# Eight more U blocks held in idle places, the residual and the group sum moved towards the end, and row shares 45, 26, 35, 30

## The chip, the cores and the metric

The kernel runs on one core of a Trainium2 chip. Its time is device microseconds of one execution, taken as the median of several runs. A profile of one further execution shows what each engine did: PE is the matrix engine (PEld its weight loads), DVE the vector engine, ACT the scalar engine, POOL the GpSimd engine, and SP the sync engine, which here only issues transfers. SPq and ACTq are the two queues from which SP and ACT issue plain transfers; gathers are issued by POOL on a third queue. A transfer stands in its engine's program like any other instruction: if the instruction ahead of it waits, it waits too.

## What is computed

One layer of a hybrid decoder over 336 tokens (16 meta tokens, 256 prompt tokens, 8 sequences of 8 new tokens): a Conformer convolution and a Mamba-2 mixer in parallel, then the PEER expert mixer, which is what the change touches.

```python
def peer_block(xb, w_q, keys, U, V):
    q = (xb @ w_q).reshape(T, PEER_HEADS, 2, D_KEY // 2)
    s = jnp.einsum('thcd,hckd->thck', q, keys)
    ...                                   # top 16 of each half, then top 16 of their sums: ids, sc
    g = jax.nn.softmax(sc, axis=-1)
    act = jax.nn.gelu(jnp.einsum('thkd,td->thk', U[ids], xb))
    return jnp.einsum('thk,thkd->td', (g * act), V[ids])
...
x = x + peer(rmsnorm(x, norm2_w), ...)    # then a last rmsnorm; 16384 experts, 8 heads x 16 experts a token
```

## The kernel before, in words

320 tokens go through the expert mixer, in two ways at once.

**Dense.** 184 tokens are multiplied with all 16384 experts. The U table is 128 blocks of 128 experts (512 KB each), the V table another 128. `u_block(b)` multiplies U block b with the tokens (8 matmuls, line 1372), and ACT writes the Gelu of the product into the table S (line 1374). The routing weights are built on the chip in 46 g steps (`g_step`): DVE makes one-hot tables `oh` (lines 1393 to 1396), PE multiplies them into a PSUM tile `pg` (line 1400), and DVE multiplies `pg` into S (line 1411). Steps 1 to 23 (half 0) serve S of blocks 0 to 63 and are mixed into U blocks 65 to 127; steps 24 to 46 serve the rest and are mixed into V blocks 0 to 63. `v_block(b)` adds V block b times S(b) to the result `va` (8 matmuls, line 1473), which stays in four PSUM tiles for the whole V part. The residual x1 is put there first, by eight matmuls with the identity (line 1442), from two ring tiles that are read back from memory. `pg` and the group sum's `pgo` share two PSUM buffers (`misc`).

**Gathered.** 128 tokens, and 8 extra tokens spread over 128 partitions, fetch their own experts. There are 136 columns: columns 0 to 63, then the 8 columns of the extra tokens, then 64 to 127. I call the work of one column a row. POOL issues a gather of 128 x 2048 numbers (1 MB, line 1125) into one of five buffers `wuv`; DVE multiplies its first half with the token (`pick_dot`, line 1273); ACT takes the Gelu and the weight (`scg`, lines 1275 and 1278); DVE adds the second half, scaled, to `ygat` or, for extra tokens, to `acce` (`pick_sum`, line 1283). When all rows of the extra tokens are in, `group_sum` adds up `acce` by two matmuls into `pgo` (line 1289).

**The order of the work.** `Feed` hands out background work (top-k searches of two token groups, g steps, rows) between the blocks, in shares fixed by NU: 46 rows while U blocks 0 to 83 run, 26 up to block 127, 36 in V blocks 0 to 63, the rest after. A scheduler then fixes one order of instructions for each engine from its own estimate of times, so that a row may stand earlier or later than its share says. On the chip every engine keeps that order and waits where it must. ACT's order mixes the Gelu of blocks, the `scg` pairs of rows, and the transfers of every second block: a transfer that stands behind an `scg` waits until DVE has made that row's product.

**The ring.** Blocks come through a ring of eight buffers, which the weights used before (`ring`, RING = 8). `bring` issues block n when block n - 8 has been used; transfers alternate between SPq and ACTq once 12 are out (line 1356). U blocks 0 to 7 are fetched earlier, into eight buffers of their own (`fetch`, line 1150), which are given up after block 7, together with the buffers of the query part. The table S of blocks 29 to 83 is later laid there.

## Time and profile before

| | us |
|---|---|
| median of 3 runs (lowest, highest) | 1314.47 (1312.41, 1314.8) |
| profiled execution, its own time | 1316.4 |
| its span | 1314.6 |
| granted PE clock, mean | 0.989 |
| PE busy, DVE busy, ACT busy, POOL busy | 1276.7, 964.2, 524.6, 574.3 |

A line of the page's groups reads: line of the kernel, engine, operation, output<-input, shapes, count | busy time, mean ns of one | idle time just before, and what ended it. A line of the timeline reads: start, duration, engine, line, operation, tiles, count of like instructions merged [idle time just before <- what ended it]. PE counts every fp32 matmul twice, so a block of eight matmuls is 16 records; on DVE a row's product counts as two instructions. A line of the windows gives the stretch, the busy time of each engine in it (with the count of instructions), the granted PE clock, the busy share of the 16 DMA engines (full at 1.02) and the GB/s moved.

### The profile page before, as it was taken

To read this page: it belongs to the slowest core of one execution; us is meant where nothing else is said; L and a number is where in the kernel's file an instruction comes from. 1 tells how busy PE (TensorE), PEld (TensorE's weight loads), DVE (VectorE), ACT (ScalarE), POOL (GpSimd) and SP (SyncE) were. 2 spreads that over 40 slices of the span, in tenths; PEclk is the share of its full clock that TensorE was granted. 3 is DMA by queue.
4 is the path that set the end of the run, shared out by engine and by line. 5 is a ranking of instruction groups with operands and counts; after the bars stand their busy time and mean duration, and the time that the engine had idled before them with its cause. 6 is when DMAs were issued, how large, how long until landed. Compare 5 with 4: busy or idle time off the path is not lost.

```text
span 1314.6 us, 23844 instructions
## 1 busy us (share of the span) xinstructions
PE 1276.7 (97%) x9015; PEld 1225.5 (93%) x9015; DVE 964.2 (73%) x2238; ACT 524.6 (40%) x1404; POOL 574.3 (44%) x504
## 2 busy tenths in 40 slices
PE   9999999999989999999998999999999899999997
PEld 7998998999879999998998998999999799999997
DVE  7888778978877245569999668888878788634444
ACT  6787877788766444544222211111111111100102
POOL 2487777787755657853122223222222222111110
PEclk9899999999999999999999999999999899999999
DMA  6434444445343444638599999999999999999992
GB/s 247 165 129 173 166 182 144 152 172 185 124 148 124 150 155 149 247 124 325 224 416 414 416 414 416 413 414 415 415 414 416 404 391 414 393 403 416 412 409 82
DMA packets 85907, 373.80 MB, mean 284 GB/s; under 512 B 10000, under 2 KB 15376, under 8 KB 66208
## 3 DMA queue, kind: packets, MB, share of 16 engines
q1 hardware_dynamic: 48048, 165.77, 33.9%
q0 software_dynamic: 19584, 142.62, 26.5%
q10 hardware_dynamic: 18160, 63.89, 12.2%
q8 instruction: 71, 1.16, 0.4%
q14 instruction: 44, 0.36, 0.1%
HBM read 359.18 MB, written 13.06 MB: 283 GB/s over the span
## 4 chain that ended last, share of the span: by engine, by line
PE 64%; DVE 15%; DMA 14%; ACT 3%; issue 2%; POOL 1%; ACTq 0%; DVEq 0%; POOLq 0%
PE pj L173 30%; PE va L1473 22%; DMA wuv<-in_peer_uv_dram,gid 13%; PE pj L1372 5%; DVE ygat L1283 2%; DVE wuv L1273 2%; PE pst L173 1%; PE po L173 1%; PE pdec L173 1%; PE pg L1400 1%; PE py L173 1%; DVE pcv L502 1%; DMA eraw<-in_uT_dram 1%; DVE cand L1090 1%; DMA wdt<-in_w_dt_dram 1%
## 5 line engine op out<-in xcount | busy, mean ns | idle before, releaser
L1125 POOL DMA_INDIRECT wuv<-in_peer_uv_dram,gid x136 | 163.4, 1201 | 506.7 <-PE va L1473 150.0
L1473 PE MATMUL va<-S,eraw 128*128 128x184 f32 x2048 | 327.1, 321 | 0.0
L241 POOL TENSOR_TENSOR wl<-wraw,wh 128x1024 fp32r<-128x1024 f32 x112 | 270.2, 2416 | 122.0 <-ACT wh L240 65.7
L1473 PEld LDWEIGHTS va<-S,eraw 128*128 128x128 f32 x2048 | 320.6, 191 | 2.6 <-issue 2.6
L1372 PE MATMUL pj<-nd,eraw 128*128 128x184 f32 x1920 | 314.1, 323 | 6.4 <-DMA eraw<-in_uT_dram 6.4
L1372 PEld LDWEIGHTS pj<-nd,eraw 128*128 128x128 f32 x1920 | 301.8, 192 | 7.9 <-issue 5.7
L173 PE MATMUL pj<-ah,wh 128*128 128x336 f32 (+1 forms) x768 | 242.4, 327 | 0.5 <-ACT xnf L216 0.4
L1283 DVE SCALAR_TENSOR_TENSOR ygat<-wuv,scg,ygat 128x1024 f32<-128x1024 f32 x128 | 164.1, 1282 | 105.3 <-ACT scg L1278 101.7
L1275 ACT ACTIVATE scg<-scg 128x1 f32<-128x1 f32 x136 | 27.1, 202 | 525.1 <-DVE wuv L1273 349.4
L173 PE MATMUL pj<-al,wh 128*128 128x336 f32 (+1 forms) x768 | 232.3, 316 | 0.0
L1273 DVE SCALAR_TENSOR_TENSOR wuv<-wuv,x2m 128x1024 f32<-128x1024 f32 x128 | 156.2, 1220 | 48.4 <-DMA wuv<-in_peer_uv_dram,gid 42.5
L240 ACT CAST wh<-wraw 128x1024 fp32r<-128x1024 f32 x125 | 131.2, 1050 | 78.9 <-PE pj L173 45.7
L502 DVE SCALAR_TENSOR_TENSOR pcv<-ccat,vec,pcv 128x256 f32<-128x256 f32 x464 | 149.3, 383 | 17.1 <-ACT pcv L500 17.1
L173 PEld LDWEIGHTS pj<-ah,wh 128*128 128x128 f32 x768 | 145.3, 190 | 6.7 <-issue 2.0
L173 PEld LDWEIGHTS pj<-al,wh 128*128 128x128 f32 x768 | 145.0, 190 | 0.9
L173 PE MATMUL pj<-ah,wl 128*128 128x336 f32 (+1 forms) x768 | 136.4, 315 | 0.7 <-POOL wl L241 0.7
L173 PEld LDWEIGHTS pj<-ah,wl 128*128 128x128 f32 x768 | 120.0, 189 | 1.1 <-POOL wl L241 1.0
L516 DVE SCALAR_TENSOR_TENSOR pj<-mcat,vec,pj 128x360 f32<-128x360 f32 x96 | 56.7, 591 | 0.7 <-ACT pj L514 0.7
L216 ACT ACT_TABLE_LOAD x39 | 50.0, 1283 | 0.7
L1374 ACT ACTIVATE S<-pj 128x184 f32<-128x184 f32 x128 | 35.9, 312 | 14.0 <-PE pj L1372 13.6
L1278 ACT ACTIVATE scg<-scg,ggw 128x1 f32<-128x1 f32 x136 | 39.6, 294 | 4.2
L1411 DVE SCALAR_TENSOR_TENSOR S<-pg,S 128x232 f32<-128x232 f32 (+1 forms) x92 | 34.5, 417 | 6.2 <-PE pg L1400 6.1
(385 smaller groups left out, 1668.6 us busy)
## 6 DMA issues: line engine op xcount, KB each, us to landing
wraw<-in_w_in_dram SPq DMA_DIRECT2D x80, 512.0 KB
eraw<-in_uT_dram SPq DMA_DIRECT2D x66, 512.0 KB
eraw<-in_vE_dram SPq DMA_DIRECT2D x64, 512.0 KB
eraw<-in_vE_dram ACTq DMA_DIRECT2D x64, 512.0 KB
eraw<-in_uT_dram ACTq DMA_DIRECT2D x54, 512.0 KB
st<-in_state_dram SPq DMA_DIRECT2D x8, 1024.0 KB
out_ssm_s_dram<-st SPq DMA_DIRECT2D x8, 1024.0 KB
wraw<-in_w_mo_dram SPq DMA_DIRECT2D x16, 512.0 KB
```

Of the source, the lines that this page charges most:

```text
L173: i_ = nc.tensor.matmul(*a_, **kw)
L216: i_ = nc.scalar.activation(out, in_, f, **kw)
L240: (nc.vector.tensor_copy if on_dve else nc.scalar.copy)(h, src)
L241: (nc.gpsimd if on_pool else nc.vector).tensor_tensor(l, src, h.bitcast(F32), op=OP.subtract)
L502: t = nc.vector.scalar_tensor_tensor(o, i_, wv, a_, op0=OP.mult, op1=OP.add)
L516: nc.vector.scalar_tensor_tensor(o, cat[:, w:w + n], wv, o, op0=OP.mult, op1=OP.add)
L1125: i_ = nc.gpsimd.indirect_dma_start(out=u, out_offset=None, in_=ia["peer_uv"], in_offset=bass.IndirectOffsetOnAxis(ap=gid[:, c:c + 1], axi ...
L1273: nc.vector.scalar_tensor_tensor(u[:, :D], u[:, :D], 1.0, x2m if c < NPICK else x2e, op0=OP.mult, op1=OP.mult, accum_out=w)
L1278: nc.scalar.activation(w, w, AF.Copy, scale=ggw[:, c:c + 1])
L1283: nc.vector.scalar_tensor_tensor(a_, u[:, D:], scg[:, c:c + 1], a_, op0=OP.mult, op1=OP.add)
L1372: i_ = nc.tensor.matmul(p[:, :ND], raw[:, k, :], nd[:, k, :], start=(k == 0), stop=(k == KD - 1))
L1473: i_ = nc.tensor.matmul(va[k // 2][:, k % 2], raw[:, k, :], Sv(b), start=False, stop=(b == 127), skip_group_check=True)
```

## The change

1. U blocks 16 to 23 go into the eight early buffers, each as soon as the block that held its place (0 to 7) has been used, and so ahead of the ring's turn. The buffers are given up after block 23 instead of block 7. All U blocks up to 24 are issued on SPq; after that odd blocks go on ACTq.
2. The residual's eight matmuls and the two loads of x1 move from the start of the V part to just before V block 104. V block 0 now starts the accumulation of `va`.
3. `group_sum` is called behind row 124 instead of row 86.
4. The shares of rows are 45, 26 and 35, and 30 remain for the V blocks from 64 on.

```diff
@@ -53,20 +53,22 @@
 SB = 84
 SA = 29
 PRE = 4
+AGAIN = 24
 HB = 64
 KTILES = ((0, NGAT), (128, 128), (256, 64))
-NU = (46, 26, 36)
+NU = (45, 26, 35)
 LM = (0.05, 0.05, 0.1, 0.5, 0.999)
 LOW = 400
 NW0 = 3
 RB = 4
 RING = RB + 4
-LATE = 12
+LATE = 24
 OH = 2
 UV = 5
 DEEP = 4
 NEAR = 2
-GLAG = 14
+GLAG = 12
+XRES = 104
 PLACE = (42, 55)
 LASTP = 126
 XW = 70
@@ -1143,10 +1145,15 @@
         fetched = []
         pres = [ExitStack(), ExitStack()]
 
+        pre_pools = []
+
+        def place_of(n):
+            return pre_pools[n // PRE].tile([128, D], F32, name="pre", tag=f"pre{n}", bufs=1)
+
         def fetch(i):
-            pp = pres[i].enter_context(tc.tile_pool(name=f"pre{i}", bufs=1))
+            pre_pools.append(pres[i].enter_context(tc.tile_pool(name=f"pre{i}", bufs=1)))
             for n in range(PRE):
-                u = pp.tile([128, D], F32, name=f"pre{i}{n}")
+                u = place_of(len(fetched))
                 nc.sync.dma_start(u, ia["uT"][len(fetched)])
                 fetched.append(u.rearrange("p (k m) -> p k m", k=KD))
 
@@ -1296,7 +1303,7 @@
                 pick_dot(n)
             if n:
                 pick_sum(n - 1)
-            if NX and n == XAT + NCOL - NPICK + GLAG:
+            if NX and n == NCOL - GLAG:
                 group_sum()
 
         ops = [(2.6, lambda n=n: pick_row(n)) for n in range(NCOL + 1)]
@@ -1339,29 +1346,41 @@
             nraw[0] += 1
             return wp.tile([128, D], F32, name="eraw", tag=tag, bufs=nb)
 
-        coming = ([("uT", b) for b in range(len(fetched), 128)] + [("x1", 0), ("x1", 5)]
-                  + [("vE", b) for b in range(128)])
+        coming = ([("uT", b) for b in range(2 * PRE, 128)] + [("vE", b) for b in range(XRES)] + [("x1", 0), ("x1", 5)]
+                  + [("vE", b) for b in range(XRES, 128)])
         landed, turn = {}, [0]
 
-        def bring(to):
-            while coming and turn[0] < to:
-                name, i = coming.pop(0)
-                raw = ring()
-                turn[0] += 1
+        def again(name, i):
+            return name == "uT" and 2 * PRE + RING <= i < AGAIN
+
+        def bring():
+            while coming:
+                name, i = coming[0]
+                if again(name, i):
+                    if len(ustep) <= i - 2 * PRE - RING:
+                        return
+                    raw = place_of(i - 2 * PRE - RING)
+                else:
+                    if turn[0] >= RING + used[0]:
+                        return
+                    raw = ring()
+                    turn[0] += 1
+                coming.pop(0)
                 if name == "x1":
                     n = min(5, KD - i)
                     raw = raw[:, :n * ND].rearrange("p (k t) -> p k t", t=ND)
                     nc.sync.dma_start(raw, x1d[:, i:i + n])
                 else:
-                    (nc.scalar if turn[0] % 2 and turn[0] > LATE else nc.sync).dma_start(raw, ia[name][i])
+                    (nc.scalar if i % 2 and (name == "vE" or i > LATE) else nc.sync).dma_start(raw, ia[name][i])
                     raw = raw.rearrange("p (k m) -> p k m", k=KD)
                 landed[name, i] = raw
 
         used = [0]
 
         def block(name, i):
-            used[0] += 1
-            bring(used[0] + RING - 1)
+            bring()
+            if not again(name, i):
+                used[0] += 1
             return landed.pop((name, i))
 
         def u_block(b):
@@ -1417,7 +1436,7 @@
         feed = Feed(bg, SB - 1)
         for b in range(SB):
             u_block(b)
-            if b == len(fetched) - 1:
+            if b == AGAIN - 1:
                 pres[1].close()
                 pres[0].close()
                 qs.close()
@@ -1434,12 +1453,13 @@
 
         va = [ps.tile([128, PJ], F32, name=f"va{a}", tag=tg, bufs=nb)[:, :2 * ND].rearrange("p (a t) -> p a t", a=2)
               for a, (tg, nb) in enumerate((("y", 2), ("y", 2), ("pb", 1), ("pj", 3)))]
-        xr = []
-        for k0, n in ((0, 5), (5, 3)):
-            r_ = block("x1", k0)
-            xr += [r_[:, k] for k in range(n)]
-        for k in (0, 1, 4, 5, 6, 7, 2, 3):
-            nc.tensor.matmul(va[k // 2][:, k % 2], ident, xr[k], start=(k % 2 == 0), stop=False, skip_group_check=True)
+        def residual():
+            xr = []
+            for k0, n in ((0, 5), (5, 3)):
+                r_ = block("x1", k0)
+                xr += [r_[:, k] for k in range(n)]
+            for k in range(KD):
+                nc.tensor.matmul(va[k // 2][:, k % 2], ident, xr[k], start=False, stop=False, skip_group_check=True)
 
         fin = []
 
@@ -1470,7 +1490,7 @@
         def v_block(b):
             raw = block("vE", b)
             for k in range(KD):
-                i_ = nc.tensor.matmul(va[k // 2][:, k % 2], raw[:, k, :], Sv(b), start=False, stop=(b == 127),
+                i_ = nc.tensor.matmul(va[k // 2][:, k % 2], raw[:, k, :], Sv(b), start=(b == 0 and k % 2 == 0), stop=(b == 127),
                                       skip_group_check=True)
                 if k == 0:
                     vstep.append(i_.ins.name)
@@ -1500,6 +1520,8 @@
         feed.drain()
         feed = Feed(take(len(ops)), LASTP - HB - 1)
         for b in range(HB, 128):
+            if b == XRES:
+                residual()
             v_block(b)
             feed.step()
             if b == LASTP:
```

The scheduler's order moves at three places on which the prediction rests.

SPq at the end of the query part (`wraw<-in_w_q` are the query weights, `pre` the early buffers, `eraw` the ring). Before:

```order
L266 DMA wraw<-in_w_q_dram 128x1024 x9
L1356 DMA eraw<-in_uT_dram 128x1024 x3
L1150 DMA pre_7404<-in_uT_dram 128x1024
L1150 DMA pre_7406<-in_uT_dram 128x1024
L1150 DMA pre_7408<-in_uT_dram 128x1024
```

Now, from the same place on:

```order
L268 DMA wraw<-in_w_q_dram 128x1024 x5
L1374 DMA pre<-in_uT_dram 128x1024
L268 DMA wraw<-in_w_q_dram 128x1024
L1374 DMA pre<-in_uT_dram 128x1024
L268 DMA wraw<-in_w_q_dram 128x1024 x3
L1374 DMA eraw<-in_uT_dram 128x1024 x3
L1157 DMA pre<-in_uT_dram 128x1024 x4
L1374 DMA eraw<-in_uT_dram 128x1024 x3
L1374 DMA pre<-in_uT_dram 128x1024
L1374 DMA eraw<-in_uT_dram 128x1024 x2
L1374 DMA pre<-in_uT_dram 128x1024 x5
```

Of the eight new loads, block 17 stands ahead of the last four query weights and block 19 ahead of the last three; block 21 and then the other five stand among the ring's first loads.

DVE between the tables of g step 4 and those of g step 5 (`wuv,scg<-wuv` is a row's product, `S<-pg` the multiplication into S, split in two). Before:

```order
L1396 TENSOR_TENSOR oh<-oh,gT 128x512 x2
L1273 SCALAR_TENSOR_TENSOR wuv,scg<-wuv,x2m 128x1024
L1283 SCALAR_TENSOR_TENSOR ygat<-wuv,scg,ygat 128x1024
L1411 SCALAR_TENSOR_TENSOR S_7608<-pg,S_7608 128x29x8
L1411 SCALAR_TENSOR_TENSOR S_7745<-pg,S_7745 128x35x8
L1393 TENSOR_TENSOR oh<-iopw,i2T 128x1024
L1394 TENSOR_TENSOR oh<-iopw,i1T 128x512
L1273 SCALAR_TENSOR_TENSOR wuv,scg<-wuv,x2m 128x1024
L1396 TENSOR_TENSOR oh<-oh,gT 128x512 x2
```

Now:

```order
L1415 TENSOR_TENSOR oh<-oh,gT 128x512 x2
L1280 SCALAR_TENSOR_TENSOR wuv,scg<-wuv,x2m 128x1024
L1290 SCALAR_TENSOR_TENSOR ygat<-wuv,scg,ygat 128x1024
L1280 SCALAR_TENSOR_TENSOR wuv,scg<-wuv,x2m 128x1024
L1290 SCALAR_TENSOR_TENSOR ygat<-wuv,scg,ygat 128x1024
L1280 SCALAR_TENSOR_TENSOR wuv,scg<-wuv,x2m 128x1024
L1290 SCALAR_TENSOR_TENSOR ygat<-wuv,scg,ygat 128x1024
L1430 SCALAR_TENSOR_TENSOR S_7608<-pg,S_7608 128x29x8
L1430 SCALAR_TENSOR_TENSOR S_8062<-pg,S_8062 128x35x8
L1412 TENSOR_TENSOR oh<-iopw,i2T 128x1024
L1413 TENSOR_TENSOR oh<-iopw,i1T 128x512
L1415 TENSOR_TENSOR oh<-oh,gT 128x512 x2
```

Counted over DVE's whole order, 35, 37, 39 and 39 row products stood ahead of the finished tables of g steps 3, 4, 5 and 6; now 36, 37, 40 and 42 do. From step 7 to step 46 the count lies between 3 below and 1 above that of before (104 and now 103 at step 46). On PE the `pg` matmuls of steps 3, 4, 5 and 6 began behind U blocks 70, 72, 75 and 79 (counted from 0); now those of step 6 begin behind block 78, the others where they did.

PE at the group sum (`pgo`; `va` is a V block, `pg` the end of a g step). Before, behind V blocks 24 and 25, in the middle of half 1:

```order
L1400 MATMUL pg<-oh 128x64
L1289 MATMUL pgo<-acce,cst 8x512
L1473 MATMUL va_10419<-S_7608,eraw 128x184 x2
L1473 MATMUL va_10420<-S_7608,eraw 128x184 x2
L1473 MATMUL va_10421<-S_7608,eraw 128x184 x2
L1473 MATMUL va_10422<-S_7608,eraw 128x184 x2
L1289 MATMUL pgo<-acce,cst 8x512
```

Now, behind the last g step:

```order
L1419 MATMUL pg<-oh 128x64
L1493 MATMUL va_10413<-S_8062,eraw 128x184 x2
L1493 MATMUL va_10414<-S_8062,eraw 128x184 x2
L1493 MATMUL va_10415<-S_8062,eraw 128x184 x2
L1493 MATMUL va_10416<-S_8062,eraw 128x184 x2
L1296 MATMUL pgo<-acce,cst 8x512 x2
```

The scheduler takes the two matmuls as soon as their two PSUM buffers come free, so they stand one V block behind g step 46 (between V blocks 59 and 60), not at row 124; on ACT, the copies out of `pgo` follow them.

## Prediction

> **What bounds the kernel now.** I read the page first, then the windows, PE's waits, and the timelines around each wait. The sizes come from the page:
>
> ```profile
> span 1314.6 us, 23844 instructions
> ...
> q0 software_dynamic: 19584, 142.62, 26.5%
> ...
> eraw<-in_uT_dram SPq DMA_DIRECT2D x66, 512.0 KB
> ```
>
> The gathers (q0) took 26.5% of the span on all DMA engines, 348.4 us, so one of the 136 costs 2.56 us of the whole DMA. A block has half a gather's bytes, so 1.28 us. Then the windows, by stretch:
>
> ```profile
> 620.00:650.00 30.00, 30.00 (x199) 30.00 (x198) 29.93 (x156) 9.88 (x32) 1.58 (x2) 1.00 0.53 193
> 650.00:700.00 50.00, 47.29 (x301) 46.50 (x299) 47.90 (x131) 10.80 (x37) 19.07 (x13) 1.00 1.02 415
> 740.00:760.00 20.00, 20.00 (x127) 19.72 (x127) 12.12 (x17) 3.85 (x17) 4.17 (x6) 0.92 1.02 415
> 800.00:820.00 20.00, 17.27 (x122) 16.78 (x121) 18.21 (x33) 4.30 (x18) 6.54 (x5) 0.91 1.02 415
> 1140.00:1287.00 147.00, 147.00 (x946) 147.00 (x945) 66.42 (x82) 13.85 (x55) 25.25 (x25) 1.00 1.00 400
> 1287.00:1303.00 16.00, 16.00 (x104) 16.00 (x104) 6.19 (x16) 4.14 (x11) 1.74 (x1) 1.00 0.10 36
> ```
>
> From 650 on the DMA is full, and PE nearly so. Only 620 to 650 has room: at a share of 0.53 of 1.02, 14 of the 30 us. At the end PE alone is the bound: 946 records in 147 us, 2.49 us for a block's 16, with the DMA done 16 us before PE. So the end moves with PE's losses, and these are few:
>
> ```profile
> PE pj L1372 <- DMA eraw<-in_uT_dram: 6.4, 6, 1.9
> PE pgo L1289 <- DVE S L1411: 5.4, 1, 5.4
> PE pg L1400 <- DVE oh L1396: 3.2, 2, 2.6
> PE va L1442 <- ACT S L1374: 1.6, 1, 1.6
> ```
>
> 16.6 us in all. The change aims at three of the four.
>
> **U blocks 16 to 23 ahead of the ring.** The six waits for U blocks look like these two on PE, and a block's transfer like this on ACT:
>
> ```profile
> 721.54 15.29 PE L1372 MATMUL pj<-nd,eraw 128*128 128x184 f32 x96 [0.95 <-DMA eraw<-in_uT_dram]
> 738.73 16.88 PE L1372 MATMUL pj<-nd,eraw 128*128 128x184 f32 x96 [1.89 <-DMA eraw<-in_uT_dram]
> ...
> 677.74 0.20 ACT L1275 ACTIVATE scg<-scg 128x1 f32<-128x1 f32 x1 [3.67 <-DVE wuv L1273]
> 677.98 0.33 ACTq L1356 DMA_DIRECT2D eraw<-in_uT_dram  x1
> ```
>
> The transfer goes out only when the row's product ahead of it on ACT is made, and DVE is full then. Eight blocks more in hand, 20 us of PE, outlast such delays, so I take all 6.4 us off. The same six blocks also took 16.88 us after the longer wait, 1.6 more than 15.29, and the window at 740 shows the clock at 0.92. So PE would come 8.0 us sooner to the g steps.
>
> The eight loads cost 10.2 us of DMA, which fits into the 14 us free before 650. On SPq, blocks 17 and 19 wait for U blocks 1 and 3, with the last four query weights queued behind them:
>
> ```profile
> 562.32 2.65 PE L1372 MATMUL pj<-nd,pre 128*128 128x184 f32 x16
> 561.10 4.23 SPq L266 DMA_DIRECT2D wraw<-in_w_q_dram  x2
> ```
>
> Both blocks are done at 564.97, and the second of these two weights, the first behind block 17, went out at 565.0 anyway. I cost this at nothing. Without that cover it costs at most the 2.65 us of these matmuls.
>
> **What is late next: the rows at the first g steps.** PE waits for DVE's tables there, and DVE for gathers:
>
> ```profile
> 794.75 0.76 DVE L1396 TENSOR_TENSOR oh<-oh,gT 128x512 f16<-128x512 f16 x2
> 803.56 0.75 DVE L1396 TENSOR_TENSOR oh<-oh,gT 128x512 f16<-128x512 f16 x2
> 810.00 0.76 DVE L1396 TENSOR_TENSOR oh<-oh,gT 128x512 f16<-128x512 f16 x2
> 813.47 0.75 DVE L1396 TENSOR_TENSOR oh<-oh,gT 128x512 f16<-128x512 f16 x2
> ...
> 795.63 0.28 PE L1400 MATMUL pg<-oh 128*128 128x64 f16 x4
> 804.04 1.17 PE L1400 MATMUL pg<-oh 128*128 128x64 f16 x16 [2.61 <-DVE oh L1396]
> 814.03 0.40 PE L1400 MATMUL pg<-oh 128*128 128x64 f16 x8
> 824.55 0.40 PE L1400 MATMUL pg<-oh 128*128 128x64 f16 x8
> ```
>
> These are g steps 3 to 6: tables ready at 795.5, 804.3, 810.8, 814.2; PE there at 795.6, 804.0, 814.0, 824.6. Step 3 had no slack, step 4 less than none. The new order puts one more row ahead of step 3, none ahead of 4, one ahead of 5 and three ahead of 6. Each costs 2.56 us of a full DMA. Against that stand the 10.2 us moved earlier, less what goes into a fuller ring, since PE and rows share one DMA. The ring can swallow nothing or all eight blocks. I take five, 6.4 us, because the rows' pace hardly answers to the ring:
>
> ```profile
> 740.00:760.00 20.00, 4.93 (x8) 0.92 1.02 415
> ```
>
> This is line 1273 alone on DVE: four rows (a row counts twice) in 20 us, beside eight PE blocks: 4 x 2.56 + 8 x 1.28 = 20.5 us of DMA, in equal halves. With fill 5 the rows' data stands 10.2 - 6.4 = 3.8 us earlier. Step by step, each ready time being the old one - 3.8 + 2.56 per added row:
>
> - Step 3 is ready at 795.5 - 3.8 + 2.6 = 794.3. PE wants it at 795.6 - 8.0 = 787.6, and waits 6.7 us. PE is 1.3 us ahead of before.
> - Step 4 is ready at 800.5. PE used to come 804.04 - 2.61 - 795.63 = 5.8 us after step 3, and comes 1.7 later for the clock after a long wait (rows below): 801.8, 2.2 ahead. The old wait of 2.61 is gone.
> - Step 5: from 804.0 to 814.0 PE took 10.0 us, of which the clock of 0.91 cost 1.8. Without that wait it comes at 801.8 + 8.2 = 810.0, step 5 being ready at 809.6: 4.0 ahead.
> - Step 6 stands one block (2.5 us) earlier in the new order, so PE comes 10.5 - 2.5 = 8.0 later, at 818.0, and it is ready at 814.2 - 3.8 + 7.7 = 818.1: still 4.0 ahead.
>
> The other wait of the 3.2 us of `pg`, 0.6 us at step 8, should go too, since fewer rows stand ahead there than before. The U part gains 4.6 us of the 8.0 aimed at.
>
> That a wait of 1.89 us is followed by a clock of 0.92 speaks about a rule of the Trainium skill. The page "TensorE: Matmul & The Clock Gate", section "Part 1: The HAM clock gate", says that TensorE falls to half clock only after an idle window of about 3.4 us; the rows after 1.89 and 2.61 us disagree, so the sum goes by the rows. By the page, step 5 would see no lost clock to win back and the sum would be 1.8 us worse.
>
> **The residual.** At the U/V boundary two rows show what is there now:
>
> ```profile
> 956.66 2.03 PE L1442 MATMUL va<-eraw,cst 128*128 128x184 f32 x12
> 960.34 0.89 PE L1442 MATMUL va<-eraw,cst 128*128 128x184 f32 x4 [1.65 <-ACT S L1374]
> ```
>
> The last two matmuls go into the second tile of `va`, which is free only when ACT has read the last U product. Six others ran first. Now V block 0 goes through the tiles in order, so two matmuls run first (0.6 us) and the second tile's wait is 1.65 + 1.3 = 2.9 us. Everything on PE, the first g steps of half 1 too, stands behind it. The eight residual matmuls only move to block 104, so the cost is 1.2 us. If ACT is in time, the edit gains the old 1.65 instead; if not, it loses up to 1.3. I take 1.2, since ACT's Gelu stood behind a row that DVE, short of DMA, had just made. The two loads move as well; they and two rows more at the end are some 7 us of DMA (2 x 2.56 + 1.8), and DMA ends 16 us ahead of PE there. Cost: nothing; without that cover up to 7.
>
> **The group sum.** Its place now and the end of the g steps:
>
> ```profile
> 1030.00 2.76 PE L1473 MATMUL va<-S,eraw 128*128 128x184 f32 x16
> 1038.12 1.86 PE L1289 MATMUL pgo<-acce,cst 128*8 128x512 f32 x2 [5.36 <-DVE S L1411]
> 1039.92 4.50 PE L1473 MATMUL va<-S,eraw 128*128 128x184 f32 x16
> ```
>
> The second matmul needs the PSUM buffer that DVE is to read for a g step, and DVE read it late, behind a row. That cost 5.36 us, and the next block took 4.50 in place of 2.76 at a lower clock: 1.74. Both are in the DVE-to-PE hand-over of one place, so the move takes off 7.1 us if the new place has no wait. There the last step's rows are:
>
> ```profile
> 1130.88 0.64 PE L1400 MATMUL pg<-oh 128*128 128x64 f16 x16
> 1131.57 0.76 DVE L1411 SCALAR_TENSOR_TENSOR S<-pg,S 128x160 f32<-128x160 f32 x2 [0.21 <-PE pg L1400]
> ```
>
> DVE has read the buffer at 1132.3. PE, after half a us of `pg`, a block of 2.5 and a first `pgo` of 0.5, needs it at 1134.4. DVE was idle and waiting for PE, so there are 2.1 us to spare and I take no wait. If a row stands in front of DVE then, as at 1038, the wait returns with its clock, up to 7.1.
>
> **The sum.** U part -4.6, boundary +1.2, group sum -7.1: -10.5 us. The profiled execution took 1316.4 us (span 1314.6 and 1.8 around it), so it becomes 1305.9. The median of the runs is 1314.47, 1.9 less: **1304.0 us**.
>
> **The rivals.** A measurement of this kernel can tell about 0.2%, 2.6 us, from no change: faster is below 1311.8, slower above 1317.1.
>
> *All 10.2 us reach the rows.* If the ring keeps no more blocks than before, rows are ready 10.2 us earlier: step 3 at 787.9 (wait 0.3), step 4 at 794.1, step 5 at 803.2, step 6 at 811.7, 10.3 us ahead of before; with step 8's wait the U part gains 10.9. Sum -10.9 + 1.2 - 7.1 = -16.8: 1297.7. For it: the ring is already bounded by its eight buffers. Against: PE's six waits for blocks show that the ring runs empty, so it has room. Chance 0.15.
>
> *The rows get nothing.* If the rows' share of the DMA is fixed at half, all eight blocks end up in the ring. Step 3 is ready at 798.1, after a wait of 10.5 us; step 4's PE comes at 805.6, step 5 at 813.8, step 6 is ready at 821.9: 0.1 ahead of before, 0.7 with step 8. Sum -0.7 + 1.2 - 7.1 = -6.6: 1307.9. For it: the equal halves from 740 to 760. Against: PE also paced these blocks, so halves may be an accident of demand. Chance 0.20. The Trainium skill, "DMA: Bandwidth & Descriptors", section "Queues, rings and completion order", has a rule of this kind: each DMA engine goes round the queues that have work, a packet at a time. The halves agree with it.
>
> *The group sum waits as before.* The new place is again behind a g step, not at row 124 as the words say. If DVE is behind there, 7.1 us come back: 1311.1. For it: the same two instructions at the same distance from a g step. Against: the 2.1 us to spare. Chance 0.15.
>
> *Slower: the added rows come at the rows' own pace.* The rows come no earlier, and one costs 20 / 4 = 5.0 us rather than 2.56. Step 3 is ready at 800.5, and step 6, three rows later, at 829.2, where PE was at 824.6 and would come 2.5 earlier: +7.1, and 1.7 for the clock: +8.8. Sum +8.8 + 1.2 - 7.1 = +2.9: 1317.4. It decides from the point where step 6's tables come after 826.3, which just eats the other two terms. For it: the same 5.0 us. Against: 8 blocks of DMA are then left unused. Chance 0.10.
>
> **How the numbers follow.** The forecast has 0.40, the rivals 0.15, 0.20, 0.15 and 0.10. Forecast and first two rivals are faster (0.75); the third lies 0.7 us below the bound, and a third of it counts as faster: 0.80. The rest of it and a third of the slower case are within 0.2%: 0.13; slower 0.07. The range leaves out the slower case and what lies beyond the ends of the others: up to 1312.0, the third rival and 0.9; down to 1296.0, the first and 1.7 for a boundary without its old wait.
>
> **What would show it.** In the new profile: DMA's share from 620 to 650 near full; PE's waits for U blocks under 1 us in all; the longest wait for `oh` about 6.7 us, at step 3 (0.3 or 10.5 for the first two rivals); a wait of about 2.9 us in V block 0; no wait at `pgo`, or one near 5 for the third rival; no `wraw` wait at the end of the query part. The prediction is wrong if waits for U blocks stay, if the query part gets longer, if PE waits at steps 5 or 6 by more than 2 us, or if the last V blocks wait for DMA.

## The result and the profile after

| | before | after |
|---|---|---|
| median of 6 runs each (lowest, highest) | 1314.63 (1312.4, 1316.59) | 1307.11 (1304.1, 1308.67) |
| profiled execution, own time | 1316.4 | 1307.06 |
| granted PE clock, mean | 0.989 | 0.992 |

The ratio is 0.9943, 95% interval 0.9927 to 0.996; a second comparison on another chip gave 0.9948 (0.9931 to 0.9966). So the change is 7.5 us faster, where 10.5 was forecast. The page's first line and PE's longest waits from the first U block on, after the change:

```profile
span 1305.3 us, 23846 instructions
```

```profile
PE pg L1419 <- DVE oh L1415: 3.9, 2, 2.3
PE pgo L1296 <- DVE S L1430: 3.7, 1, 3.7
PE pj L1391 <- DMA eraw<-in_uT_dram: 3.0, 4, 1.8
...
PE pj L1391 <- ACT S L1393: 2.4, 2, 1.5
```

These four hold 13.0 us, where the four of before held 16.6. The waits for U blocks, for `oh` and at `pgo` are still there; only the 1.6 us ahead of the residual's last two matmuls are gone, and `oh` has 3.9 us where it had 3.2. The wait for ACT S is one by name alone: both blocks behind it landed 0.13 us before their use, as the block behind the longest of the named DMA waits did, and the Gelu that had to free their PSUM buffers was done over 4 us earlier. So these 2.4 us belong to the U blocks too, 5.4 in all. Six stretches, the first four those of before:

```profile
620.00:650.00 30.00, 30.00 (x198) 30.00 (x197) 29.93 (x150) 8.90 (x29) 3.26 (x3) 1.00 0.76 274
650.00:700.00 50.00, 47.99 (x307) 47.49 (x306) 48.46 (x131) 13.06 (x46) 19.39 (x14) 1.00 0.95 363
740.00:760.00 20.00, 20.00 (x137) 19.64 (x136) 10.93 (x13) 3.26 (x14) 4.38 (x5) 1.00 1.02 415
800.00:820.00 20.00, 17.60 (x130) 17.16 (x129) 18.18 (x34) 4.34 (x17) 6.00 (x5) 0.91 1.02 415
1140.00:1280.00 140.00, 140.00 (x901) 140.00 (x900) 64.61 (x79) 13.42 (x54) 27.68 (x25) 1.00 1.01 408
1283.00:1294.00 11.00, 11.00 (x73) 11.00 (x72) 5.21 (x13) 2.89 (x7) 1.74 (x1) 1.00 0.15 52
```

The head start went out: the DMA's share between 620 and 650 rose from 0.53 to 0.76. But from 650 to 700 it fell from full to 0.95. At the end PE is still nearly alone: in its last 11 us the share is 0.15.

To see where the time went, I line up the starts of the same blocks on PE's timeline (us; the end is the last V matmul):

| | to U0 | U0 to U112 | U112 to V0 | V0 to V66 | V66 to end | U0 to end |
|---|---|---|---|---|---|---|
| before | 547.3 | 366.9 | 46.9 | 187.8 | 154.8 | 756.3 |
| after | 545.0 | 364.4 | 42.6 | 185.1 | 157.2 | 749.3 |

U0 is the first U block on PE, V0 the first V block. The first column is not the change's. Nothing that it issues stands before U0 on PE, and over the 14 profiles of this study (most with the same instructions there) that stretch took 545.0 to 549.3 us, in no order that follows the edits. So I compare from U0 on, where the change is worth 7.0 us: 2.5 in the U part, 4.3 at the U/V boundary less 2.5 for the residual's new place, 2.7 up to V66.

### The profile page after: what moved, and what is told of

It reads as the page before. It is cut to its first block, busy times and chain, and to the rows that moved or that the text cites. A ratio compares the mean times of both kernels' runs of the same rounds, so it can differ in the third digit from the quotient of the medians.

```text
span 1305.3 us, 23846 instructions
## 1 busy us (share of the span) xinstructions
PE 1272.7 (98%) x9015; PEld 1222.5 (94%) x9015; DVE 962.5 (74%) x2238; ACT 527.4 (40%) x1404; POOL 583.5 (45%) x504
## 4 chain that ended last, share of the span: by engine, by line
PE 73%; DVE 13%; DMA 8%; ACT 3%; issue 1%; POOL 1%; ACTq 0%; DVEq 0%; POOLq 0%
PE pj L175 30%; PE va L1493 23%; PE pj L1391 11%; DMA wuv<-in_peer_uv_dram,gid 8%; DVE ygat L1290 2%; DVE wuv L1280 2%; PE pg L1419 1%; PE pst L175 1%; PE po L175 1%; PE pdec L175 1%; PE py L175 1%; DVE pcv L504 1%; ACT L218 1%; DMA wdt<-in_w_dt_dram 1%; DVE si L1048 1%
## 5 line engine op out<-in xcount | busy, mean ns | idle before, releaser
L1127 POOL DMA_INDIRECT wuv<-in_peer_uv_dram,gid x136 | 171.9, 1264 | 493.7 <-PE va L1493 148.1
L1391 PE MATMUL pj<-nd,eraw 128*128 128x184 f32 x1792 | 293.0, 322 | 5.5 <-DMA eraw<-in_uT_dram 3.0
L1391 PEld LDWEIGHTS pj<-nd,eraw 128*128 128x128 f32 x1792 | 280.4, 191 | 7.7 <-ACT S L1393 3.8
L1280 DVE SCALAR_TENSOR_TENSOR wuv<-wuv,x2m 128x1024 f32<-128x1024 f32 x128 | 156.5, 1223 | 45.6 <-DMA wuv<-in_peer_uv_dram,gid 45.1
L1391 PE MATMUL pj<-nd,pre 128*128 128x184 f32 x256 | 41.9, 319 | 0.0
## 6 DMA issues: line engine op xcount, KB each, us to landing
eraw<-in_uT_dram SPq DMA_DIRECT2D x60, 512.0 KB, 10.5
```

The costliest lines, as they stand in the source:

```text
L1127: i_ = nc.gpsimd.indirect_dma_start(out=u, out_offset=None, in_=ia["peer_uv"], in_offset=bass.IndirectOffsetOnAxis(ap=gid[:, c:c + 1], axi ...
L1280: nc.vector.scalar_tensor_tensor(u[:, :D], u[:, :D], 1.0, x2m if c < NPICK else x2e, op0=OP.mult, op1=OP.mult, accum_out=w)
L1391: i_ = nc.tensor.matmul(p[:, :ND], raw[:, k, :], nd[:, k, :], start=(k == 0), stop=(k == KD - 1))
```

## The experiments

Each row below is a kernel; the ratio is against the kernel before, on the same chip; the columns are PE's stretches as above.

| kernel | ratio (95%) | U0 to U112 | U112 to V0 | V0 to V66 | V66 to end | U0 to end |
|---|---|---|---|---|---|---|
| changed, again | 0.9948 (0.9931 to 0.9966) | 364.7 | 42.6 | 185.4 | 157.2 | 749.8 |
| sum at its old place | 0.9931 (0.9917 to 0.9945) | 363.8 | 42.6 | 185.9 | 157.2 | 749.5 |
| sum behind V block 99 | 0.9926 (0.9913 to 0.9939) | 364.4 | 42.6 | 177.6 | 161.7 | 746.2 |
| U supply of before | 0.9970 (0.9959 to 0.998) | 367.4 | 47.2 | 179.6 | 157.2 | 751.4 |
| U blocks all on SPq | 0.9937 (0.992 to 0.9955) | 366.0 | 42.6 | 179.6 | 157.2 | 745.4 |
| shares 42, 27, 36 | 0.9904 (0.9886 to 0.9922) | 362.1 | 42.6 | 181.1 | 158.1 | 743.9 |
| residual first | 0.9944 (0.9928 to 0.996) | 364.6 | 45.1 | 185.3 | 154.8 | 749.7 |
| sum behind V99, shares 42, 27, 36 | 0.9899 (0.988 to 0.9918) | 363.8 | 42.6 | 177.7 | 161.3 | 745.3 |
| shares of before | 0.9965 (0.9954 to 0.9976) | 366.5 | 42.5 | 185.6 | 157.2 | 751.8 |
| before, shares 42, 27, 36 only | 0.9939 (0.9924 to 0.9955) | 366.3 | 44.9 | 180.7 | 154.9 | 746.7 |
| sum behind V62 | 0.9913 (0.99 to 0.9927) | 362.8 | 42.6 | 180.5 | 158.7 | 744.5 |
| sum behind V62, shares 42, 27, 36 | 0.9905 (0.9889 to 0.9922) | 365.8 | 42.6 | 179.7 | 158.1 | 746.2 |

The ratios come from 5 to 12 runs each, the stretches from one profile each. How far a stretch repeats can be read from kernels in which every engine has the same work in the same order up to U block 112, but for at most 16 places on ACT. U0 to U112 took 362.8 to 364.7 us in the six of them with the shares 45, 26, 35 and the new U supply on two queues, and 362.1, 363.8 and 365.8 in the three with the new supply and 42, 27, 36. So a difference of 2 or 3 us in that column, between two single profiles, shows little by itself. V0 to V66 repeats better: 185.1, 185.4 and 185.3 in the changed kernel, the same again, and with the residual first. Where I compare with the changed kernel's ratio, I take 0.9945, the middle of its two comparisons.

### The group sum: old place, tied to the end, tied just behind

**Old place.**

```diff
-            if NX and n == NCOL - GLAG:
+            if NX and n == XAT + NCOL - NPICK + 14:
```

> The changed kernel with only the group sum called behind row 86 again; both of its matmuls then stand together behind V block 27, in the middle of half 1. The traces of the two kernels, lined up block by block, say that the old place cost 10.6 us between V blocks 24 and 30 and the new one 7.5 us between V blocks 54 and 66, so the move gained 3.1. Theory A (the second matmul waits wherever a g step stands just ahead, since DVE reads that step's buffer only behind rows that wait for gathers): a wait for S of 2 to 6 us comes back at the old place and the time is 1 to 5 us above the changed kernel's 1307.1. Theory B (the prediction: the old place costs 7.1 and the new one nothing): 7 us above, 1314.

The time did not rise; the runs are even a little faster than the changed kernel's, inside both intervals. PE's timeline has the wait, at the old place:

```profile
1030.61 1.02 PE L1296 MATMUL pgo<-acce,cst 128*8 128x512 f32 x2
1034.74 1.86 PE L1296 MATMUL pgo<-acce,cst 128*8 128x512 f32 x2 [3.11 <-DVE S L1430]
1036.54 3.74 PE L1493 MATMUL va<-S,eraw 128*128 128x184 f32 x11
```

So B is out. A has the wait, but not its 1 to 5 us: V0 to V66 takes 185.9 here and 185.1 to 185.4 in the changed kernel, so the move as it was made is worth under 1 us. In the changed kernel the same picture stands at the new place. PE first, then DVE:

```profile
1114.65 1.03 PE L1296 MATMUL pgo<-acce,cst 128*8 128x512 f32 x2
1119.42 1.04 PE L1296 MATMUL pgo<-acce,cst 128*8 128x512 f32 x2 [3.75 <-DVE S L1430]
```

```profile
1112.30 1.28 DVE L1290 SCALAR_TENSOR_TENSOR ygat<-wuv,scg,ygat 128x1024 f32<-128x1024 f32 x1 [0.60 <-ACT scg L1285]
1115.50 1.22 DVE L1280 SCALAR_TENSOR_TENSOR wuv<-wuv,x2m 128x1024 f32<-128x1024 f32 x1 [1.91 <-DMA wuv<-in_peer_uv_dram,gid]
1116.65 0.08 DVE L1280 DVE_READ_ACCUMULATOR wuv<-wuv,x2m 128x1 f32 x1
1117.33 1.28 DVE L1290 SCALAR_TENSOR_TENSOR ygat<-wuv,scg,ygat 128x1024 f32<-128x1024 f32 x1 [0.60 <-ACT scg L1285]
1118.53 0.75 DVE L1430 SCALAR_TENSOR_TENSOR S<-pg,S 128x160 f32<-128x160 f32 x2
```

The last g step's `pg` was done at 1112.1, but DVE's program has a whole row ahead of the product that reads it, and that row waited 1.91 us for its gather. DVE read the buffer at 1119.3, and the second `pgo` could go.

**Tied behind V block 99, and behind V block 62.** Both tie the two matmuls behind a given V block:

```diff
-                nc.tensor.matmul(p[:NX], C(f"sel{NX}"), acce[:, cs], start=True, stop=True)
+                after(nc.tensor.matmul(p[:NX], C(f"sel{NX}"), acce[:, cs], start=True, stop=True), vstep[-1])
```

The second kernel has `vstep[62]` in place of `vstep[-1]`.

> The changed kernel with the two matmuls of the group sum tied behind the newest V block at the time of the call, which puts them between V blocks 99 and 100, where no g step is left; the order of DVE and SP is unchanged. Theory A: the 3.75 us wait and the 1.72 us that the next blocks lost at a lower clock both go, PE ends 5.5 us earlier, 1301.6. Theory C (the end is set by something else by now, the last rows or the DMA, which stops some 11 us ahead of PE in the changed kernel): the wait goes but the time stays within 1.5 us of 1307.1.

> The changed kernel with the group sum's two matmuls tied behind V block 62, three blocks after their place, past the last g step's product; the order of DVE and SP is the same, ACT's differs in 16 lines. Theory A: the wait of 3.7 to 4.0 us (in the three profiles of this order) and its clock go, and unlike the tie behind block 100, which took 2.4 us back through late V blocks, nothing else moves: V blocks 54 to 102 take 123.0 us in place of 128.4 to 128.7, and the ratio falls by 0.004, to 0.990 or 0.991. Rival (what PE gains here it loses to late V blocks, since the DMA is full): V blocks 66 to 102 take 2 us more than 89.8, ratio 0.9925.

In the first, the wait went and V0 to V66 fell by 7.5 us, 2.1 of them only because the two matmuls moved out of it. V66 to the end grew by 4.5: the two matmuls' 2.1, and 2.4 more. Of these, 1.1 us are two waits for V blocks, the larger shown here; most of the rest is small delays, under 0.11 us each, at every second block, for which the profile names no cause:

```profile
1133.46 16.79 PE L1493 MATMUL va<-S,eraw 128*128 128x184 f32 x105 [0.88 <-DMA eraw<-in_vE_dram]
```

The net was 3.1 us by the profile, between A's 5.5 and C's nothing. In the second kernel, three blocks behind their place, the two matmuls found both buffers free:

```profile
1111.49 0.64 PE L1419 MATMUL pg<-oh 128*128 128x64 f16 x16
1111.97 10.22 PE L1493 MATMUL va<-S,eraw 128*128 128x184 f32 x64
1122.12 1.88 PE L1296 MATMUL pgo<-acce,cst 128*8 128x512 f32 x4
```

V54 to V102 took 122.9 us (123.0 expected, 128.4 to 128.7 in the changed kernel), and the ratio fell from 0.9945 to 0.9913. Some 1.5 us came back late, behind V block 102, 0.7 of them in a named wait for a V block. So A has the place and the size, and the rival is right that a little of it is lost to late blocks. Of the 4.8 us from U0 to the end, 1.6 are in the U part, which this edit does not touch.

### The supply of U blocks

**As before.** Places not used twice (`AGAIN = 16`, early buffers closed after block 7), even blocks from 20 on issued by ACT.

```diff
-                    (nc.scalar if i % 2 and (name == "vE" or i > LATE) else nc.sync).dma_start(raw, ia[name][i])
+                    (nc.scalar if (i % 2 if name == "vE" else i % 2 == 0 and i > 19) else nc.sync).dma_start(raw, ia[name][i])
```

> The changed kernel with only the supply of U blocks as before: no second use of the early buffers, even blocks from 20 on issued by ACT. Theory D (from block 32 on every block again has just the ring's eight blocks of lead, so the head start only shifts some DMA work ahead of 650 us and brings the rows about 3 us forward): U waits like before, about 6 us in all, and the time 1 to 3 us above 1307.1. Theory B (the head start outlasts the delays of ACT's queue): the U part loses 4.6 us, 1311.7. Theory E (the U part is paced by the rows alone): same time within 1 us.

The ratio of 0.9970 is 3.3 us above the changed kernel's 0.9945, just past D's upper end; B's 4.6 lies inside the intervals too, but not by its mechanism: PE waited 6.1 us in front of U blocks against 5.5, as D has it. But the edit moved more than the supply. The scheduler made another order of DVE with it: ahead of g steps 3 to 6 stand 35, 37, 39 and 39 rows, as in the kernel before. The rows also stood later (row 24, counted from 0, started at 740.7 in place of 735.8), and at g step 19, with 62 rows ahead of its tables in place of 59, PE met a new wait:

```profile
920.28 1.29 PE L1419 MATMUL pg<-oh 128*128 128x64 f16 x16 [2.28 <-DVE oh L1415]
921.39 3.77 PE L1391 MATMUL pj<-nd,eraw 128*128 128x184 f32 x16
```

By the profile the U part and the boundary took 7.6 us longer (3.0 and 4.6), and V0 to V66 gave 5.5 back, because there was no wait at the group sum. So the 3.3 us belong to the whole new order, and not to the head start alone.

Why the waits stay is seen at the longest of them in the changed kernel, ACT's row first, then PE's:

```profile
689.94 0.33 ACTq L1374 DMA_DIRECT2D eraw<-in_uT_dram  x1
```

```profile
698.39 15.20 PE L1391 MATMUL pj<-nd,eraw 128*128 128x184 f32 x96 [1.84 <-DMA eraw<-in_uT_dram]
```

This is U block 37. Its place had been free since block 29 ended at 678.7; ACT got to the transfer 11 us later, behind the `scg` pairs of four rows and 3.0 us of other work. It was no exception: of the blocks 32 to 71, SP's even ones went out as soon as their place was free, ACT's odd ones 5.2 to 12.2 us later. All blocks up to 31 were out by 644, but block 32 needs the place of block 24 and went out at 666.3, when that block was used, and so on: from there on the ring is just eight blocks deep again. The head start does not travel along, and in the 22 us without a new block the DMA's share fell to 0.95.

**All on SPq.**

```diff
-                    (nc.scalar if i % 2 and (name == "vE" or i > LATE) else nc.sync).dma_start(raw, ia[name][i])
+                    (nc.scalar if i % 2 and name == "vE" else nc.sync).dma_start(raw, ia[name][i])
```

> The changed kernel with all U blocks issued by SP, so that none stands behind a row's scg on ACT; the order of PE is unchanged. Theory D: the waits for U blocks (3.0 us by name, 2.4 more put down to ACT S where a block landed 0.13 us before its use) go, under 1 us is left. What that is worth tells D from E: if the rows pace PE, the waits at the first g steps grow by the same 5 us and the time stays at 1307 within 1.5 us; if the waits for blocks themselves cost, the time falls by 3 to 5 us, to 1303.

D fell here: no U block stands behind an `scg` now, blocks 32 to 71 all went out as soon as their place was free, and PE waits for U blocks more often than ever, while the waits for `oh` vanish.

```profile
PE pj L1391 <- DMA eraw<-in_uT_dram: 10.3, 12, 1.2
```

The queues show it. From 735 to 780, of the changed kernel and of this one (packets, MB, share):

```profile
q0 software_dynamic: 1399, 10.20, 55.1%
q1 hardware_dynamic: 1245, 4.51, 25.1%
q10 hardware_dynamic: 1083, 3.91, 21.4%
```

```profile
q0 software_dynamic: 1561, 11.35, 61.0%
q1 hardware_dynamic: 2021, 7.36, 40.9%
```

q0 are the gathers, q1 and q10 the queues of SP and ACT. With one queue in place of two, the blocks' part fell from 46.5% to 40.9%, though all were asked for in time, and the gathers got the difference. The page "DMA: Bandwidth & Descriptors" of the Trainium skill, section "Queues, rings and completion order", says that a DMA engine goes round the queues that have work, packet by packet. An estimate from that rule, with the mean packets of these rows (7.3 KB for a gather, 3.6 KB for a block) as its packets, is half for two block queues and one third for one. The trace agrees in direction only: the blocks' part fell, but by much less. So late issue was only one face of a DMA that is full: U0 to U112 came out 366.0 us long, above the 362.8 to 364.7 of the six kernels named above, and the runs are not clearly faster than the changed kernel's. V0 to V66 is 5.5 us shorter in this profile, as in the one before it, because the wait at the group sum is missing there. The order of PE is that of the changed kernel, and DVE's differs in three places: the rows came in another phase. Whether the wait is missing in all six runs (1304.7 to 1310.6 us) is not known.

### The rows ahead of the tables

**Shares 42, 27, 36** in the changed kernel, and then as the only edit of the kernel before (there in place of 46, 26, 36):

```diff
-NU = (45, 26, 35)
+NU = (42, 27, 36)
```

> The changed kernel with row shares 42, 27 and 36: 35, 36, 37 and 38 row products stand ahead of the tables of g steps 3 to 6 in place of 36, 37, 40 and 42; PE's order of U blocks and g steps is the same. Theory F (the gathers that DVE's order puts ahead of the tables are what PE pays for; fewer of them, fewer waits): the waits for oh fall from 3.9 us to under 1, no block after step 5 runs at a lower clock, and the U part is 2 to 4 us shorter: 1303 to 1305. Theory G (blocks and rows share one full DMA, so that a row less only moves the wait to U blocks or to the end): the same time within 1 us.

> The kernel before with nothing but the row shares 42, 27 and 36: no head start, residual first, group sum behind row 86. The rows ahead of g steps 3 to 6 fall from 35, 37, 39 and 39 to 35, 36, 37 and 38. Theory F: the 2.6 us at step 4 and the 1.8 us of its lower clock go, waits for U blocks stay at 6 to 8 us, and the ratio is 0.994 to 0.997, most of what the whole change brought. Theory H (the head start is what allows it; without it the DMA has no room and U blocks wait longer by the same amount): 0.998 to 1.001.

In the changed kernel F has the waits: none for `oh` is left, and the ratio is 0.9904, 5.4 us below the changed kernel's. But the gain is not where F put it. Of the 5.9 us by the profile (749.8 to 743.9, against the second profile of the changed kernel) 4.3 are between V0 and V66, where the wait at the group sum fell to 1.3 us with no block at a lower clock; 2.6 are in the U part, and 0.9 was lost behind V66. The 2.6 did not repeat: the two kernels below with the same order there took 363.8 and 365.8 us. In the U part G has it right, since U blocks are late now, one of them where step 5 was:

```profile
PE pj L1391 <- DMA eraw<-in_uT_dram: 7.1, 5, 3.2
...
PE pgo L1296 <- DVE S L1430: 1.3, 1, 1.3
```

The same line alone on the kernel before brought it to 0.9939, as far as all four parts of the change together, a little past what F gave and well off H. Its waits:

```profile
PE pj L1372 <- DMA eraw<-in_uT_dram: 8.7, 4, 3.1
...
PE pgo L1289 <- DVE S L1411: 0.9, 1, 0.9
```

F expected the gain at step 4, and its wait is gone; but waits for U blocks took that place, and U0 to U112 is only 0.6 us shorter. The gain is at the boundary (2.0) and in V0 to V66 (7.1). The wait at the boundary is gone; that at the group sum fell from 5.4 us to 0.9, at a place that the scheduler moved along, from behind V blocks 24 and 25 to behind V block 30. The parts are not independent: each moves the rows against PE's program, and with them every wait that hangs on a row.

**Shares of before** in the changed kernel (46, 26, 36):

> The changed kernel with only the row shares 46, 26 and 36 of before. Up to g step 7 the same number of rows stands ahead of the tables as in the changed kernel, from step 8 on about one more (44 for 43 at step 8, 103.5 for 102.5 at step 46). Theory F (a row costs only where it stands ahead of a table that PE is about to need): steps 8 to 46 have 5 to 12 us to spare in the changed kernel, so one more row of 5 us or less changes nothing, and the time is within 1.5 us of the changed kernel, 0.9930 to 0.9960 of before. Rival (every row in the U part costs its 2.56 us of DMA): 2 to 4 us slower, above 0.9965.

F fell here. The ratio, 0.9965, is 2.6 us above the changed kernel's: the rival's time, at its lower bound, but not by its mechanism, since the cost stands in two places. One part is in the U part (step 18, with 60 rows ahead in place of 58, waits 1.2 us); the larger is in V block 0, where V0 to V24 takes 69.9 us in place of 65.4. In the table the group sum hides it, which waited only 0.7 us here. PE's timeline, then ACT's:

```profile
956.90 0.46 PE L1419 MATMUL pg<-oh 128*128 128x64 f16 x10
960.26 1.17 PE L1493 MATMUL va<-S,eraw 128*128 128x184 f32 x4 [2.90 <-ACT S L1393]
```

```profile
955.20 0.52 ACT L1393 ACTIVATE S<-pj 128x184 f32<-128x184 f32 x2
959.47 0.20 ACT L1282 ACTIVATE scg<-scg 128x1 f32<-128x1 f32 x1 [3.76 <-DVE wuv L1280]
959.71 0.29 ACT L1285 ACTIVATE scg<-scg,ggw 128x1 f32<-128x1 f32 x1
...
959.91 0.30 ACT L1393 ACTIVATE S<-pj 128x184 f32<-128x184 f32 x1
```

The Gelu of the last U block stands behind a row's `scg`, the second tile of `va` behind that Gelu: the 2.9 us that the prediction gave for this place, but under the old shares.

**Both cures together.** The tie behind V99 and the tie behind V62, each with shares 42, 27, 36.

> Group sum tied behind V block 100 and row shares 42, 27, 36 together. If both cures act on waits of their own, they add up: 1302 to 1303, the fastest so far. If DMA has become the bound of the end (the tied kernel showed waits of 1.1 us for V blocks, and its V blocks 66 to 102 took 2.3 us more than in the changed kernel), the later rows take it back and the time stays at 1305 to 1306.

> The changed kernel with the group sum tied behind V block 62 and row shares 42, 27 and 36. With fewer rows the wait at the group sum was 1.3 us with no block at the lower clock, so the tie can win only about 1.3 us beyond the shares alone: ratio 0.989 (the shares alone gave 0.9904). Rival: the later rows make V blocks late, as in the tie behind block 100: 0.990 to 0.991.

0.9899 and 0.9905 beside 0.9904 for the shares alone: the cures do not add up, since with these shares the wait at the group sum was nearly gone. In both, waits for U blocks were longer (9.5 and 9.7 us with those under another name, against 7.6), though the order of the U part is the same: that is the spread of single profiles. The first loses 2 us behind V66 again. All three are faster than both kernels, and none is clearly the fastest.

### The residual, and the changed kernel again

The residual's matmuls and loads back ahead of V block 0:

> The changed kernel with only the residual at the start of the V part again, its loads ahead of the V blocks. By the two traces the move gained 1.9 us (4.4 at the boundary, 2.5 given back at block 104): 1309. By the prediction it cost 1.2 us, so that undoing it would give 1306.

0.9944, the changed kernel's own time. PE's timeline has no wait at the boundary:

```profile
954.24 2.66 PE L1462 MATMUL va<-eraw,cst 128*128 128x184 f32 x16
956.73 2.66 PE L1495 MATMUL va<-S,eraw 128*128 128x184 f32 x16
```

The 2.5 us of the matmuls stand at the boundary instead of at block 104, and that is all. So neither side was right: the 1.9 us that the traces show there were the old Gelu wait, which the new shares took away, not the move.

> The changed kernel once more, beside the next three. The first two profiles say that the stretch before the first U block differs by up to 3 us between executions of the same instructions (545.0 to 548.1), and that the wait at the group sum's new place was 3.75 us in the changed kernel but absent in the two kernels that changed only the U supply. Theory A (that wait depends on how the rows happen to fall, a matter of a few us of DVE): it may be absent here too, and V blocks 24 to 66 then take 114 us in place of 119.7. Rival: it belongs to this order of instructions and comes back at 3 to 4 us. Time 1307 within 1.5 us either way.

The wait at the group sum came back at 4.0 us, and V24 to V66 took 119.9; with the residual first it was 3.7. So it belongs to this kernel, and the rival has it. The order of PE and DVE alone does not make it: with all U blocks on SPq that order is the same but for three places, and there was no wait.

## Why the prediction was right, and where its steps were not

The direction and the range were right: 1304.0 was forecast, 1307.1 measured, and the end moved with PE's waits as said. The mechanism was right in part. Two of the prediction's own signs of being wrong came true: the waits for U blocks stayed, and PE waited more than 2 us at step 5. That the time came out so near is in part luck, since errors of both signs met. Four of its steps failed.

- **"Eight blocks more in hand, 20 us of PE, outlast such delays, so I take all 6.4 us off."** 5.4 of the 6.4 stayed. The blocks in hand are spent at block 31, and the late transfers begin behind it. That step mistook one early delivery for a deeper ring. What the head start did give is 10.2 us of DMA work moved ahead, of which the rows got 2 to 4 us (rows 24 to 30 start 5.3 to 6.9 us earlier, 3.2 of it from the front and U block 4): around the 3.8 that a fill of five blocks gave. The 1.6 us of clock at 738 were won, since the wait there went.
- **The steps.** Step 3 was ready at 792.5, 0.5 us from the forecast if PE's earlier front of 2.3 is taken off; but PE came late by the U waits that stayed, so that its wait was 1.6 us and not 6.7. At step 5, forecast without a wait, PE waited 2.27 us and lost 1.7 to the clock. DVE in the rows between the tables of steps 4 and 5, then the finished tables of step 5; below them PE at step 5:

```profile
799.27 1.28 DVE L1290 SCALAR_TENSOR_TENSOR ygat<-wuv,scg,ygat 128x1024 f32<-128x1024 f32 x1 [0.60 <-ACT scg L1285]
800.47 1.22 DVE L1280 SCALAR_TENSOR_TENSOR wuv<-wuv,x2m 128x1024 f32<-128x1024 f32 x1
...
802.29 1.28 DVE L1290 SCALAR_TENSOR_TENSOR ygat<-wuv,scg,ygat 128x1024 f32<-128x1024 f32 x1 [0.60 <-ACT scg L1285]
803.50 1.22 DVE L1280 SCALAR_TENSOR_TENSOR wuv<-wuv,x2m 128x1024 f32<-128x1024 f32 x1
...
808.24 0.76 DVE L1415 TENSOR_TENSOR oh<-oh,gT 128x512 f16<-128x512 f16 x2
```

```profile
808.72 0.61 PE L1419 MATMUL pg<-oh 128*128 128x64 f16 x5 [2.27 <-DVE oh L1415]
```

No row waits for its gather here: each takes 3.0 us on DVE, 0.6 of it waiting for ACT's `scg`. I priced an added row by its gather, 2.56 us; here DVE's own chain was the longer. The U part gave 2.5 us in place of 4.6.
- **"the second tile's wait is 1.65 + 1.3 = 2.9 us", a cost of 1.2.** The mechanism and size are what the kernel with the old shares shows. With shares 45 and 26 ACT is in time and the old 1.65 goes as well: a gain of 1.9, beyond the 1.65 given as the other bound. The step failed in taking the state of ACT over from the old trace, although the same change moves a row there.
- **"DVE was idle and waiting for PE, so there are 2.1 us to spare and I take no wait."** The wait was 3.75 us, and 1.7 of clock: the rival in which the group sum waits as before, at three quarters of its size (5.5 of 7.1). The slack was read from the old order, where PE came to step 46 at 1130.9, 10 us after its tables; PE is at 1111.5 now and DVE, 3.3 us after the tables, in the middle of a row. V0 to V66 gave 2.7 us in place of 7.1.

Two gains were forecast too large (U part and group sum, 6.5 us together), and the boundary came out 3.1 us better than forecast. That leaves the 3.4 us between -10.5 and -7.1 from U0 on; without the 3.1 the change would have brought 4.0 us by the profile. What was forecast at nothing cost nothing that can be told from the spread of the front: the new waits on SPq, and the later rows at the end. On the clock, the page "TensorE: Matmul & The Clock Gate" of the Trainium skill, section "Part 1: The HAM clock gate", has the clock fall to half after an idle window of about 3.4 us. This case's rows do not agree: the new ones again show a lower clock after 2.27 us.

Open is what the head start is worth by itself. With shares 45, 26, 35 the kernel without it is 3.3 us slower, and with 42, 27, 36 the kernel before reaches 0.9939 and the changed one 0.9904; but in both pairs the order of DVE differs too, and in the second also the places of the residual and of the group sum. No run keeps the order of the rows and takes the head start away alone. Other combinations were not tried.

## What to carry to other kernels

A wait that hangs on a row of background work is a matter of phase: moving the instruction that waits, or the rows, moves it to the next place where PE runs close behind DVE, so read its slack from the order as it will be, not as it was. Before work is rearranged around such waits, try how much of the background work stands ahead of them: one line of shares did here what the whole change did. And buffers that are filled early once give a head start, not depth.

## What the runs showed of the hardware

- Between 735 and 780 us two queues of blocks beside one of gathers held 46.5% of the DMA, one queue 40.9%, at the same total.
- A wait of PE between 1.9 and 2.7 us in the U and V parts is sometimes followed by a lower clock and sometimes not: after 1.89, 2.03, 2.08, 2.27 and 2.61 us some ten matmul records started 307 ns apart in place of 156 (1.5 to 1.8 us lost), after 1.97, 2.00, 2.31 and 2.60 us none did. After waits up to 1.84 us it was not seen; after all ten waits of 2.9 us and more it was. In the changed kernel the granted clock was 0.50 from 809.7 to 813.1 us and full in the 3.4 us on either side.
- The same instructions ahead of U0 took between 545.0 and 549.3 us in the profiles, a spread of 4.3 us, over half of what the change is worth.
